# One layer of a retention and S5 decoder: projections' tail in the two-bank layout, the last pair without GpSimd additions, retention's first loads on ACT's queue

## The chip, the cores and the metric

The kernel runs on one core of one Trainium2 chip. The metric is the device time of one execution in microseconds (us), as the median of several runs. The engines are TensorE (PE in the profile, with its weight loads as PEld), VectorE (DVE), ScalarE (ACT), GpSimd (POOL) and SyncE (SP). SP, ACT and POOL each have a queue of their own for issuing transfers (DMAs).

## What is computed

One layer over 1032 tokens (1024 of a prompt, 8 single-token samples), in float32, width 2048:

```python
h = rmsnorm(x, g_pre)
q, k, v, za, ub, zb, ga, gb = split(h @ w_in)             # 2048 -> 6 x 1024 and 2 x 2048 columns
ya, s_ret_new = retention(q, k, v, pos, s_ret)            # 8 heads, chunks of 128
ya = (ya * silu(za)) @ w_pa
yb, s_re, s_im = s5(ub, ...)                              # diagonal SSM, gelu, GLU
yb = (yb * silu(zb)) @ w_pb
merged = sigmoid(ga) * ya + sigmoid(gb) * yb
out = merged @ w_out
y = x + rmsnorm(out, g_post)
```

## The kernel before

Everything on TensorE is float32-accurate: an operand is split into a high part (`whi`, the rounded copy, cast by ACT) and a low part (`wlo`, the difference, on DVE), and each product is the three matmuls high x high, high x low, low x high. Weights come in 256 KB quarters (128 x 512) on SP's queue.

**Block products (line 892).** The larger projections go by pairs of 128-row blocks, each pair by seven products (n = 0 to 6) of 24 matmuls with 258 columns. A product accumulates in an `acc` tile, which is two PSUM banks wide; there are three of them (pool `pst`, six banks) and two `misc` banks (pool `pms`). Of a step's seven products n=0 and n=2 share one tile, n=1, 3 and 5 another, n=4 and 6 the third. `evac_st` and `evac_p` empty them by ACT copies and DVE additions; results are called "11", "22", "21", "12". In the last stage, `w_pb` (kind "pb", p = 0 to 7), `gated` multiplies a result by its gate (`zz`), adds the part of `w_pa` (`pap_d`, in DRAM), and writes to `mg_d`. The addition has two forms: an ACT load of the part (`pp`) in `load_z` and an addition by an engine, or an accumulating DMA from `pap_d` onto the tile on POOL's queue and, LAG = 4 products later, the write to `mg_d`. For p > 1 it is the first form, on DVE, except p = 7, where "11", "22" and "21" are added by POOL.

**Retention (lines 1011 to 1100).** Its heads are worked off in slots between the block products of `w_in`'s last pairs. `ret_const` loads constants by POOL's queue (`col`, `mask`, `selr`), sets `mhalf` on DVE and casts `selr` to `sel` on DVE. Head 0's first transfers (`load_vk`: `vT`, 516 KB, and `kT`, two of 258 KB) are issued by POOL's queue when `head(0)` starts. PE transposes `vT` through `misc` banks (lines 1046 and 1049), and ACT copies them out (line 1047) and so frees the banks.

**Output projection (line 1620 on).** `psum_layout(("pmm", 5), ("pms", 3))` closes the PSUM pools of the block products and opens one of five single banks (`mm`) and one of three (`misc`). `out_rows` computes 16 row blocks of the last 392 tokens (the 48 matmuls of a block have 392 columns, lines 209 to 211). `out_tokens` computes five column blocks of 128 tokens (`c`), three in a first call and two in a second (`last`), in four groups (`g`) of 512 output columns: per group 16 steps k, in each of which every column does its three matmuls (line 1782); then `evac` takes each column: a Square with a sum on ACT (line 1725), and a product with the gain on DVE (`z<-mm`). An `out_rows` load of the merged rows (`z<-mg_d`, line 1651) is issued by ACT's queue.

The order on each engine is set by a scheduler that goes through the program with estimated times, so an edit can move neighbours on the same engine. Tiles are released as a whole: who writes a tile anew waits for every reader of its last use, and closing a pool waits for all of its tiles.

Of the kernel before, what the change touches and what calls it, by code (L numbers as in the profile page):

```python
# [10 lines left out]
F32 = mybir.dt.float32  # L11
# [10 lines left out]
TOK = SEQ + NB  # L22
# [56 lines left out]
def emit(ctx, tc, I, O):  # L79
    nc = tc.nc  # L80
    V, A, P, T = nc.vector, nc.scalar, nc.gpsimd, nc.tensor
# [7 lines left out]
    def add(out, a, b, eng=None):  # L89
        return tt(out, a, b, ALU.add, eng)  # L90
# [22 lines left out]
    def psum_layout(*pools):  # L113
        if "stack" in banks_of:
            banks_of.pop("stack").close()
            banks_of.clear()
        st = banks_of["stack"] = ExitStack()
        for name, bufs in pools:
            banks_of[name] = st.enter_context(tc.tile_pool(name=name, bufs=bufs, space=PSUM))
# [93 lines left out]
    def mmbank(name="mm"):  # L213
        if "pst" in banks_of:
            return banks_of["pst"].tile([128, 2, 512], F32, name="acc")[:, 0, :]
        return banks_of["pmm"].tile([128, 512], F32, name="mm")

    def misc():
        return banks_of["pms"].tile([128, 512], F32, name="misc")
# [657 lines left out]
    acc = {}  # L877
# [130 lines left out]
    K = {}  # L1008

    def ret_const():  # L1010
        for n, shape in (("col", [128, 4, H]), ("mask", [128, 128])):
            K[n] = rp.tile(shape, F32, name=n)
            P.dma_start(K[n], I[n])
        K["mhalf"] = rp.tile([128, 8], F32, name="mhalf")
        V.memset(K["mhalf"], -0.5)
        selr = rp.tile([128, 64], F32, name="selr")
        P.dma_start(selr, I["sel"])
        K["sel"] = rp.tile([128, 8, 8], F32R, name="sel")
        V.tensor_copy(K["sel"], selr.rearrange("p (b c) -> p b c", b=8))
        K["a"] = act.tile([128, 2, TOK], F32, name="a12")  # L1020
        K["b"] = act.tile([128, 2, TOK], F32, name="a13")

    R = lambda name, shape, bufs=1, dt=F32: rp.tile(shape, dt, name=name, bufs=bufs)

    def load_vk(h):
        vT, kT = R("vT", [128, TOK]), R("kT", [128, TOK], 2)
        P.dma_start(vT, v_d[h])
        for a in range(2):
            P.dma_start(kT[64 * a:64 * a + 64], kq_d[0, h // 2, a, 64 * (h % 2):64 * (h % 2) + 64])
        return vT, kT  # L1030

    def head(h):
# [1 line left out]
        sq = lambda t: t[:, 0:1024].rearrange("p (a b) -> p a b", a=8)  # L1034
        qT, st = K["a"][:, 0], sq(K["a"][:, 1])
        vt, s0 = sq(K["b"][:, 0]), sq(K["b"][:, 1])
        vT, kT = K.pop("next") if h else load_vk(h)
        for a in range(2):
            P.dma_start(qT[64 * a:64 * a + 64], kq_d[1, h // 2, a, 64 * (h % 2):64 * (h % 2) + 64])
        if not h:  # L1040
# [445 lines left out]
    def load_z(s, name):  # L1486
        kind, p = steps[s]
        r, c = AT[name]
        zq[name] = zz_tile()
        A.dma_start(zq[name], (sga_d if kind == "pa" else sgb_d)[2 * p + r, :, HT * c:HT * c + HT])  # L1490
        if kind == "pb" and p > 1:
            zq[name, "p"] = ppp.tile([128, HT], F32, name="pp")
            A.dma_start(zq[name, "p"], pap_d[2 * p + r, :, HT * c:HT * c + HT])

    def gated(g, name, t, ps=None):
        s = g // 7
        kind, p = steps[s]
        r, c = AT[name]
        m, cols = 2 * p + r, slice(HT * c, HT * c + HT)
        z = zq.pop(name)  # L1500
        if ps is None:
            mul(t, t, z)
        else:
            mul(two(t), ps, two(z))
        if kind == "pa":
            P.dma_start(pap_d[m, :, cols], t)
        elif (name, "p") in zq:
            add(t, t, zq.pop((name, "p")), P if p == 7 and name != "12" else V)
            if c and p > 5:
                last_t[m] = t  # L1510
            P.dma_start(mg_d[m, :, cols], t)
        else:
            P.dma_start(t, pap_d[m, :, cols], accum_op=ALU.add)
            at(g + LAG, lambda: P.dma_start(mg_d[m, :, cols], t))
# [104 lines left out]
    estack.close()  # L1619
    wstack.close()  # L1620
    stage_pool(SW, 3)
    psum_layout(("pmm", 5), ("pms", 3))
    zp = ctx.enter_context(tc.tile_pool(name="zp", bufs=1))
    stl = ctx.enter_context(tc.tile_pool(name="stl", bufs=2))
    wxp = ctx.enter_context(tc.tile_pool(name="wxp", bufs=1))
# [79 lines left out]
    def out_tokens(c0, nch, last):  # L1705
        if last:
            view = lambda t: t.rearrange("p (k c) -> p k c", k=4)
            more.extend(view(st_tile()) for _ in range(2))
        zt, slots, sm = {}, {}, {}
        zts[last] = zt  # L1710
        S = 512
        for c in range(nch):
            o = 8 * (c0 + c)
            sm[c] = small[:, o:o + 4], small[:, o + 4:o + 5], small[:, o + 5:o + 6], small[:, o + 6:o + 7]

        def x_of(g, c):
            o = (nch + (c if last else 0)) * S
            return zt[g][:, o:o + S]

        def load_x(g, c):  # L1720
            P.dma_start(x_of(g, c), I["xB"][c0 + c, :, S * g:S * g + S])

        def evac(g, c, ps):
            s4, r1, r2, r3 = sm[c]
            A.activation(misc(), ps, AF.Square, accum_out=s4[:, g:g + 1])
            mul(zt[g][:, c * S:c * S + S], ps, gb[:, S * g:S * g + S])
            if g == 2:
                add(r1, s4[:, 0:1], s4[:, 1:2])
                add(r1, r1, s4[:, 2:3])
                V.tensor_scalar(r1, r1, 1.0 / D, EPS, ALU.mult, ALU.add)  # L1730
                V.memset(r2, -0.5)
            if g == 3:
                V.scalar_tensor_tensor(r1, s4[:, 3:4], 1.0 / D, r1, ALU.mult, ALU.add)
                P.tensor_tensor(r3, r1, r2, ALU.pow)

        def finish(g, c, eng, x=None):
            z = zt[g][:, c * S:c * S + S]
            V.scalar_tensor_tensor(z, z, sm[c][3], x_of(g, c) if x is None else x, ALU.mult, ALU.add)
            eng.dma_start(O["yB"][c0 + c, :, S * g:S * g + S], z)

        RING = [0, 1, 2, 3, 1, 2, 3, 2, 3, (0,), (1,), 3]

        def place(i):
            p = RING[i]
            return zts[True][0][:, (2 + p[0]) * S:(3 + p[0]) * S] if isinstance(p, tuple) else zt[p][:, 3 * S:4 * S]

        def load_step(i):
            P.dma_start(place(i), I["xB"][c0 + i % 3, :, S * (i // 3):S * (i // 3) + S])  # L1750

        def finish_all():
            then = {1: (4,), 2: (5,), 3: (6,), 4: (9,), 5: (7, 10), 6: (8,), 8: (11,)}
            for i in range(12):
                g, c = divmod(i, 3)
                for _ in range(4):
                    yield
                finish(g, c, P, place(i))
                for n in then.get(i, ()):
                    load_step(n)  # L1760
                if i in (9, 10):
                    P.dma_start(place(i), I["xB"][c0 + 3 + i - 9, :, 0:S])
                if c == 2:
                    free.append(slots[g])

        order_w = deque((g, k) for g in range(4) for k in range(KD))
        w = {}
        for g in range(4):
            ps = [mmbank() if c < 2 else misc() for c in range(nch)]
            steps = [[(k, c) for c in range(nch)] for k in range(KD)]  # L1770
            if last and g == 3:
                steps[13:] = [[(k, c) for k in (13, 14, 15)] for c in range(nch)]
            for st in steps:
                for k, c in st:
                    while order_w and order_w[0] <= (g, k + 1):
                        gk = order_w.popleft()
                        w[gk] = wtile(I["w_outB"][gk])
                    wh, wl = (t.rearrange("p a b -> p (a b)") for t in w[g, k])
                    t = (c0 + c) * 128
                    xh, xl = (a[:, t:t + 128] for a in mg[k])  # L1780
                    for a, b in ((xh, wh), (xh, wl), (xl, wh)):
                        anchor["p"] = T.matmul(ps[c], a, b, start=k == 0 and a is xh and b is wh, stop=k == KD - 1 and a is xl).ins  # L1782
                    if k == KD - 1:
                        if c == 0:
                            slots[g] = free.popleft()
                            zt[g] = flat(slots[g])
                            if not last:
                                load_step(g)
                            elif g:
                                for cc in range(nch):  # L1790
                                    load_x(g, cc)
                        evac(g, c, ps[c])
                        if last and g == 3:
                            for gg in range(4):
                                finish(gg, c, A if gg % 2 else nc.sync)
                slot()
        if not last:
            bg.append(finish_all())
# [85 lines left out]
```

## Time and profile before

| what | us |
|---|---|
| median of 3 runs | 2610.0 (2609.98 to 2617.08) |
| profiled execution | 2613.67 |
| its span on the core | 2611.9 |
| PE busy | 2588.0 (99%) |
| DVE busy | 1856.4 (71%) |
| ACT busy | 956.0 (37%) |
| POOL busy | 688.8 (26%) |

The span is the time from the core's first to its last instruction in the profiled execution; 1.8 us of that execution lie outside it. The profile's page lists busy time by engine, the chain that ended last, and the costliest groups of instructions; the trace answers for any stretch what each engine ran, what it waited for (in square brackets behind an instruction: idle time before it and who released it), and the clock that TensorE was granted (1.00 is full speed).

### The profile page before, as it was taken

What the parts mean: (1) busy time and instruction counts of PE and PEld (TensorE: products, weight loads), DVE (VectorE), ACT (ScalarE), POOL (GpSimd) and SP (SyncE); (2) the same over time, 40 slices, a digit from 0 to 9 for tenths busy, and PEclk for the clock granted to TensorE, in tenths of its full rate; (3) what the DMA queues carried; (4) which work ended last, traced back from release to release, by engine and by line L of the source; (5) the groups of instructions that cost most, each with busy time, mean ns of one, the idle gap of its engine ahead of it and who ended that gap; (6) DMA issues with size and microseconds to landing.
All of it is one profiled execution on the core that took longest, in us unless ns stands there. A gap on an engine that the chain in (4) does not pass through costs nothing.

```text
span 2611.9 us, 51326 instructions
## 1 busy us (share of the span) xinstructions
PE 2588.0 (99%) x19652; PEld 2531.1 (97%) x19652; DVE 1856.4 (71%) x3872; ACT 956.0 (37%) x1679; POOL 688.8 (26%) x1137
## 2 busy tenths in 40 slices
PE   9999999999999999999999999999999999999998
PEld 8999999999999999999999999999999999998886
DVE  7655988898898877558877666666577878544555
ACT  6113232333323324443234444445332422443344
POOL 0103322222222222332234434333422221111011
PEclk9999999999999999999999999999999999999999
DMA  6896534444444447886778878778867786655666
GB/s 192 257 265 217 154 111 125 138 120 124 129 122 131 131 127 245 207 206 168 164 192 241 231 197 209 206 196 250 273 226 255 232 230 212 215 166 182 187 200 227
DMA packets 229909, 500.25 MB, mean 192 GB/s; under 512 B 32432, under 2 KB 54912, under 8 KB 229536
## 3 DMA queue, kind: packets, MB, share of 16 engines
q0 software_dynamic: 90352, 263.82, 36.2%
q1 hardware_dynamic: 103072, 179.57, 22.5%
q10 hardware_dynamic: 36240, 53.60, 7.0%
q8 instruction: 154, 2.52, 0.4%
q14 instruction: 91, 0.75, 0.1%
HBM read 340.57 MB, written 156.30 MB: 190 GB/s over the span
## 4 chain that ended last, share of the span: by engine, by line
PE 97%; DVE 1%; issue 1%; DMA 1%; ACT 0%; DVEq 0%; SPq 0%; POOLq 0%; POOL 0%; ACTq 0%
PE acc L892 65%; PE mm L1782 7%; PE mm L209 5%; PE mm L210 5%; PE mm L211 5%; PE misc L1782 2%; PE acc L209 1%; PE acc L210 1%; PE acc L211 1%; PE misc L634 1%; PE misc L712 1%; PE misc L711 1%; PE misc L1099 1%; PE misc L1089 1%; PE misc L1068 1%
## 5 line engine op out<-in xcount | busy, mean ns | idle before, releaser
L892 PE MATMUL acc<-a,whi 128*128 128x258 f32 x9632 | 1561.4, 284 | 1.0 <-ACT whi L873 0.6
L892 PEld LDWEIGHTS acc<-a,whi 128*128 128x128 f32 x9632 | 1325.8, 190 | 5.2 <-issue 2.6
L892 PE MATMUL acc<-a,wlo 128*128 128x258 f32 x4816 | 969.1, 282 | 0.0
L892 PEld LDWEIGHTS acc<-a,wlo 128*128 128x128 f32 x4816 | 744.7, 189 | 0.0
L84 DVE TENSOR_TENSOR wlo<-wraw,whi 128x512 fp32r<-128x512 f32 x482 | 332.0, 689 | 237.9 <-ACT whi L202 138.1
L873 ACT CAST whi<-wraw 128x512 fp32r<-128x512 f32 x344 | 213.5, 621 | 619.6 <-PE acc L892 481.1
L873 ACT CAST whi<-wr 128x512 fp32r<-128x512 f32 x258 | 160.0, 620 | 507.4 <-PE acc L892 445.3
L209 PE MATMUL mm<-a,whi 128*128 128x384 f32 (+2 forms) x704 | 234.2, 334 | 8.6 <-ACT whi L202 5.2
L210 PE MATMUL mm<-a,whi 128*128 128x384 f32 (+2 forms) x704 | 233.7, 332 | 0.0
L211 PE MATMUL mm<-a,wlo 128*128 128x384 f32 (+2 forms) x704 | 232.2, 330 | 0.0
L84 DVE TENSOR_TENSOR wlo<-wr,whi 128x512 fp32r<-128x512 f32 x273 | 187.2, 686 | 51.6 <-ACT whi L873 30.0
L1782 PE MATMUL mm<-whi,a 128*128 128x512 f32 x512 | 171.1, 395 | 0.0
L202 ACT CAST whi<-wraw 128x512 fp32r<-128x512 f32 x138 | 85.5, 620 | 208.2 <-PE mm L210 104.1
L209 PEld LDWEIGHTS mm<-a,whi 128*128 128x128 f32 x704 | 133.6, 190 | 9.2 <-ACT whi L202 5.2
L211 PEld LDWEIGHTS mm<-a,wlo 128*128 128x128 f32 x704 | 133.9, 190 | 0.4 <-DVE wlo L84 0.2
L210 PEld LDWEIGHTS mm<-a,whi 128*128 128x128 f32 x704 | 133.3, 189 | 0.4 <-DVE a L363 0.4
L84 DVE TENSOR_TENSOR wraw<-wr 128x512 f32<-128x512 f32 x172 | 118.1, 686 | 2.9 <-DMA wr<-in_w_pa 0.6
L1782 PEld LDWEIGHTS mm<-whi,a 128*128 128x128 f32 x512 | 96.1, 188 | 22.8
L84 DVE TENSOR_TENSOR p<-acc,p 128x516 f32<-128x516 f32 x86 | 59.6, 692 | 70.9 <-PE acc L892 70.7
L84 DVE TENSOR_TENSOR wlo<-wx,whi 128x512 fp32r<-128x512 f32 x76 | 52.5, 692 | 71.4 <-ACT whi L202 71.1
L84 DVE TENSOR_TENSOR u<-acc,u 128x516 f32<-128x516 f32 x86 | 59.7, 694 | 60.0 <-PE acc L892 58.7
L84 DVE TENSOR_TENSOR u<-acc,p 128x516 f32<-128x516 f32 x86 | 59.5, 692 | 59.0 <-PE acc L892 58.7
(374 smaller groups left out, 3449.3 us busy)
## 6 DMA issues: line engine op xcount, KB each, us to landing
wr<-in_w_in SPq DMA_DIRECT2D x280, 256.0 KB
pt_d<-u POOLq DMA_DIRECT2D x70, 258.0 KB, 3.2
u<-pt_d POOLq DMA_DIRECT2D x70, 258.0 KB, 5.3
wraw<-in_w_outB SPq DMA_DIRECT2D x66, 256.0 KB
stg<-fm_d POOLq DMA_DIRECT2D x44, 258.0 KB, 4.5
wx<-in_w_outB SPq DMA_DIRECT2D x43, 256.0 KB
wraw<-in_w_out SPq DMA_DIRECT2D x39, 256.0 KB
pt_d<-st POOLq DMA_DIRECT2D x35, 258.0 KB, 3.3
```

The source lines that it names most:

```text
L84: return (eng or V).tensor_tensor(out, a, b, op)
L202: anchor["a"] = A.copy(hi, raw).ins
L209: T.matmul(ps, wh[:, i, :], xh[:, t0:t1], start=first, stop=False)
L210: T.matmul(ps, wh[:, i, :], xl[:, t0:t1], start=False, stop=False)
L211: anchor["p"] = T.matmul(ps, wl[:, i, :], xh[:, t0:t1], start=False, stop=last).ins
L634: T.matmul(ps[0:16, g * 128:(g + 1) * 128], B1[:, g, :], W3[:, g, 0:8, :], start=True, stop=True)
L711: T.matmul(o, Tm[:, g, :], U[:, g, 0:136], start=True, stop=False)
L712: T.matmul(o, W3[:, g, 1:9, :], X[:, g, 0:136], start=False, stop=True)
L873: anchor["a"] = A.copy(hi, f).ins
L892: anchor["p"] = T.matmul(ps[:, j, 0:258], a[:, i, :], b[:, 258 * j:258 * j + 258], start=first and i == 0 and a is wh and b is xh, stop=n ...
L1068: T.matmul(ps[:, c * 128:(c + 1) * 128], kt[:, 4 * i + c, :], vt[:, 4 * i + c, :], start=True, stop=True)
L1782: anchor["p"] = T.matmul(ps[c], a, b, start=k == 0 and a is xh and b is wh, stop=k == KD - 1 and a is xl).ins
```

## The change

Three edits.

1. Retention: `ret_const` allocates `a12` and `a13` first and issues head 0's `vT` and `kT` loads, by ACT's queue; `head(0)` takes them from there. On POOL's queue the three transfers are gone from behind `selr`.
2. Last pair (p = 7) of the "pb" products: "11" and "21" have no `pp` load any more and take the accumulating DMA on POOL's queue, with the write to `mg_d` four products later; "22" is added on DVE, as "12" was.
3. Output projection: the PSUM pools stay as they were (three `acc` tiles of two banks, two `misc` banks). In `out_rows` a block uses one bank of an `acc` tile. In `out_tokens` columns 0 and 1 share an `acc` tile, and column 2 has one of its own; in the first call the last two steps (k = 14, 15) go column by column; in the last group of the second call column 1 has its own tile.

```diff
     def ret_const():
+        K["a"] = act.tile([128, 2, TOK], F32, name="a12")
+        K["b"] = act.tile([128, 2, TOK], F32, name="a13")
+        K["next"] = load_vk(0, A)
         for n, shape in (("col", [128, 4, H]), ("mask", [128, 128])):
...
         V.tensor_copy(K["sel"], selr.rearrange("p (b c) -> p b c", b=8))
-        K["a"] = act.tile([128, 2, TOK], F32, name="a12")
-        K["b"] = act.tile([128, 2, TOK], F32, name="a13")
...
-    def load_vk(h):
+    def load_vk(h, eng=P):
         vT, kT = R("vT", [128, TOK]), R("kT", [128, TOK], 2)
-        P.dma_start(vT, v_d[h])
+        eng.dma_start(vT, v_d[h])
         for a in range(2):
-            P.dma_start(kT[64 * a:64 * a + 64], kq_d[0, h // 2, a, 64 * (h % 2):64 * (h % 2) + 64])
+            eng.dma_start(kT[64 * a:64 * a + 64], kq_d[0, h // 2, a, 64 * (h % 2):64 * (h % 2) + 64])
...
-        vT, kT = K.pop("next") if h else load_vk(h)
+        vT, kT = K.pop("next")
...
-        if kind == "pb" and p > 1:
+        if kind == "pb" and p > 1 and (p < 7 or c):
             zq[name, "p"] = ppp.tile([128, HT], F32, name="pp")
...
-            add(t, t, zq.pop((name, "p")), P if p == 7 and name != "12" else V)
+            add(t, t, zq.pop((name, "p")), V)
...
-    psum_layout(("pmm", 5), ("pms", 3))
...
-            ps = [mmbank() if c < 2 else misc() for c in range(nch)]
+            both_ = banks_of["pst"].tile([128, 2, 512], F32, name="acc")
+            ps = [both_[:, 0, :], both_[:, 1, :]]
+            if nch == 3:
+                ps.append(mmbank())
             steps = [[(k, c) for c in range(nch)] for k in range(KD)]
             if last and g == 3:
+                ps[1] = mmbank()
                 steps[13:] = [[(k, c) for k in (13, 14, 15)] for c in range(nch)]
+            elif not last:
+                steps[14:] = [[(k, c) for k in (14, 15)] for c in range(nch)]
```

How this moves instructions, at three places. On DVE where retention starts, before (`u_16992` is product n=1's result, `u_17059` that of n=3; the `wlo` behind `mhalf` is the low half of n=3's weights):

```order
L84 TENSOR_TENSOR wlo<-wr,whi 128x512
L1015 MEMSET mhalf 128x8
L84 TENSOR_TENSOR wlo<-wraw,whi 128x512
L84 TENSOR_TENSOR wraw<-wr,wraw 128x512
L84 TENSOR_TENSOR wraw<-wr 128x512
L84 TENSOR_TENSOR u_16992<-p_16932,acc 128x516
L84 TENSOR_TENSOR wlo<-wraw,whi 128x512
L84 TENSOR_TENSOR wraw<-wraw,wr 128x512
L1019 CAST sel<-selr 128x64
L84 TENSOR_TENSOR wlo<-wr,whi 128x512
```

The same place after:

```order
L84 TENSOR_TENSOR wlo<-wr,whi 128x512
L1018 MEMSET mhalf 128x8
L84 TENSOR_TENSOR u_16992<-p_16932,acc 128x516
L1022 CAST sel<-selr 128x64
L84 TENSOR_TENSOR wlo<-wraw,whi 128x512
L84 TENSOR_TENSOR wraw<-wr,wraw 128x512
L84 TENSOR_TENSOR wlo<-wraw,whi 128x512
L84 TENSOR_TENSOR wraw<-wr 128x512
L84 TENSOR_TENSOR wlo<-wr,whi 128x512
```

The low half of n=3's weights stood ahead of the cast of `selr` and now stands behind it.

On PE where the output projection starts, with the semaphores that an instruction waits for, before:

```order
L892 MATMUL acc<-a_26229,whi 128x258 x4
L892 MATMUL acc<-a_26229,wlo 128x258 x2
L209 MATMUL mm<-a_27795,whi 128x392 [waits DVE_49,Activation_49]
L210 MATMUL mm<-a_27795,whi 128x392
L211 MATMUL mm<-a_27795,wlo 128x392
L209 MATMUL mm<-a_27836,whi 128x392
```

The same place after:

```order
L892 MATMUL acc<-a_26229,whi 128x258 x4
L892 MATMUL acc<-a_26229,wlo 128x258 x2
L209 MATMUL acc<-a_27795,whi 128x392 [waits PE_49,Activation_49]
L210 MATMUL acc<-a_27795,whi 128x392
L211 MATMUL acc<-a_27795,wlo 128x392 [waits DVE_49]
L209 MATMUL acc<-a_27836,whi 128x392
```

The order is the same; the first matmul's wait for DVE is gone, and the third has one, for its own `wlo`.

On PE at the end of the first `out_tokens` group, before (`mm_29419`, `mm_29420` and `misc_29421` are columns 0, 1 and 2; a14 and a15 are the steps k = 14 and 15):

```order
L1782 MATMUL misc_29421<-whi_29671,a14_28123 128x512
L1782 MATMUL mm_29419<-whi_29687,a15_28120 128x512
L1782 MATMUL mm_29419<-wlo_29688,a15_28120 128x512
L1782 MATMUL mm_29419<-whi_29687,a15_28120 128x512
L1782 MATMUL mm_29420<-whi_29687,a15_28120 128x512
L1782 MATMUL mm_29420<-wlo_29688,a15_28120 128x512
L1782 MATMUL mm_29420<-whi_29687,a15_28120 128x512
```

After (`acc_29407` holds columns 0 and 1, `acc_29408` column 2, `acc_29715` the next group's columns 0 and 1):

```order
L1788 MATMUL acc_29407<-whi_29674,a15_28115 128x512
L1788 MATMUL acc_29408<-whi_29658,a14_28118 128x512
L1788 MATMUL acc_29408<-wlo_29659,a14_28118 128x512
L1788 MATMUL acc_29408<-whi_29658,a14_28118 128x512
L1788 MATMUL acc_29408<-whi_29674,a15_28115 128x512
L1788 MATMUL acc_29408<-wlo_29675,a15_28115 128x512
L1788 MATMUL acc_29408<-whi_29674,a15_28115 128x512
L1788 MATMUL acc_29715<-whi_29719,a0_27795 128x512
L1788 MATMUL acc_29407<-whi_29658,a14_28118 128x512
L1788 MATMUL acc_29407<-wlo_29659,a14_28118 128x512
L1788 MATMUL acc_29407<-whi_29658,a14_28118 128x512
```

Between column 0's last matmul (the first row) and column 1's steps k = 14 and 15, which write the tile that column 0's evacuation reads, there are now six matmuls of column 2 and one of the next group.

## Rows read from the trace of the kernel before

**Rows 1.** The page: PE's busy time, and the chain that ended last by engine.

```profile
PE 2588.0 (99%) x19652; PEld 2531.1 (97%) x19652; DVE 1856.4 (71%) x3872; ACT 956.0 (37%) x1679; POOL 688.8 (26%) x1137
PE 97%; DVE 1%; issue 1%; DMA 1%; ACT 0%; DVEq 0%; SPq 0%; POOLq 0%; POOL 0%; ACTq 0%
```

**Rows 2.** What PE waited for, by line of the waiting instruction: us in total, times, longest. The other entries are of 0.6 us and less.

```profile
PE mm L209 <- ACT whi L202: 5.2, 1, 5.2
PE mm L209 <- DVE u L84: 2.8, 1, 2.8
PE misc L1049 <- ACT a L1047: 2.2, 1, 2.2
```

**Rows 3.** PE where retention starts: start us, duration us, instruction, and in brackets the idle time before it and its releaser.

```profile
1361.51 0.65 PE L892 MATMUL acc<-a,whi 128*128 128x258 f32 x4
1362.00 0.40 PE L892 MATMUL acc<-a,wlo 128*128 128x258 f32 x2
1362.23 0.64 PE L892 MATMUL acc<-a,whi 128*128 128x258 f32 x4
1365.11 0.27 PE L1049 MATMUL misc<-ident,vT 128*8 128x128 f32 x1 [2.23 <-ACT a L1047]
```

**Rows 4.** ACT in the same stretch.

```profile
1346.04 0.58 ACT L982 COPY p<-acc 128x516 f32<-128x516 f32 x1
...
1362.65 1.28 ACT L966 ACT_TABLE_LOAD   x1 [2.16 <-DMA st<-pt_d]
...
1364.49 1.06 ACT L1047 COPY a<-misc 128x512 f32<-128x512 f32 x2
```

**Rows 5.** DVE in the same stretch.

```profile
1347.47 0.07 DVE L1015 MEMSET mhalf<- 128x8 f32 x1 [3.35 <-DMA kq_d<-pl]
1347.54 0.69 DVE L84 TENSOR_TENSOR wlo<-wraw,whi 128x512 fp32r<-128x512 f32 x1
...
1352.67 0.20 DVE L1019 CAST sel<-selr 128x64 fp32r<-128x64 f32 x1 [1.06 <-DMA selr<-in_sel]
1352.78 0.68 DVE L84 TENSOR_TENSOR wlo<-wr,whi 128x512 fp32r<-128x512 f32 x1
1354.36 0.70 DVE L84 TENSOR_TENSOR u<-acc,p 128x516 f32<-128x516 f32 x1 [0.89 <-PE acc L892]
```

**Rows 6.** DMA issues of 1336 to 1366 us: tiles, queue, count, KB each, median us from issue to landing.

```profile
kq_d<-pl POOLq DMA_DIRECT2D x3, 258.0 KB, 4.7
...
vT<-v_d POOLq DMA_DIRECT2D x1, 516.0 KB, 6.9
...
st<-pt_d POOLq DMA_DIRECT2D x1, 258.0 KB, 9.9
...
selr<-in_sel POOLq DMA_DIRECT2D x1, 32.0 KB, 3.7
```

**Rows 7.** Four stretches by window: from and to, length, busy us (instructions) of PE, PEld, DVE, ACT and POOL, granted clock, DMA share, GB/s. They are the stretch of rows 3, the idle time ahead of the output projection, its first matmuls, and one in the middle of `out_tokens`.

```profile
1360.00:1366.00 6.00, 3.77 (x33) 3.56 (x32) 1.57 (x3) 3.37 (x5) 1.39 (x3) 1.00 1.01 294
2231.80:2234.80 3.00, 0.24 (x2) 0.03 (x1) 3.00 (x5) 1.04 (x2) 2.08 (x2) 1.00 0.07 26
2234.80:2238.60 3.80, 3.73 (x12) 3.76 (x13) 2.81 (x5) 0.00 (x0) 0.54 (x1) 0.55 0.65 215
2450.00:2500.00 50.00, 50.00 (x218) 40.52 (x217) 18.85 (x33) 16.75 (x31) 0.54 (x1) 1.00 0.48 137
```

**Rows 8.** PE where the output projection starts, columns as in rows 3.

```profile
2231.64 0.40 PE L892 MATMUL acc<-a,wlo 128*128 128x258 f32 x2
2234.87 0.48 PE L209 MATMUL mm<-a,whi 128*128 128x392 f32 x1 [2.83 <-DVE u L84]
...
2238.64 0.34 PE L209 MATMUL mm<-a,whi 128*128 128x392 f32 x1
2238.81 0.34 PE L210 MATMUL mm<-a,whi 128*128 128x392 f32 x1
```

**Rows 9.** DVE ahead of that place and at it.

```profile
2224.65 1.04 DVE L84 TENSOR_TENSOR a<-mga,a 128x392 fp32r<-128x392 f32 x2
...
2228.13 2.14 DVE L84 TENSOR_TENSOR a<-mga,a 128x392 fp32r<-128x392 f32 x2
...
2232.36 1.76 DVE L84 TENSOR_TENSOR wlo<-wraw,whi 128x512 fp32r<-128x512 f32 x1
2234.04 0.68 DVE L84 TENSOR_TENSOR u<-acc,u 128x516 f32<-128x516 f32 x1
```

**Rows 10.** POOL and ACT there: the last addition on POOL, ACT's issue of the loads of merged rows, and ACT's first evacuation of `out_rows`.

```profile
2232.05 1.52 POOL L84 TENSOR_TENSOR p<-p,pp 128x516 f32<-128x516 f32 x1 [1.35 <-DVE p L84]
...
2241.31 0.85 ACTq L1651 DMA_DIRECT2D z<-mg_d  x2
...
2245.63 0.49 ACT L1675 ACTIVATE sp<-mm 128x392 f32<-128x392 f32 x1
```

**Rows 11.** The page's DMA issues, columns as in rows 6: the accumulating transfers of the block products (onto `u`, from `pt_d`).

```profile
u<-pt_d POOLq DMA_DIRECT2D x70, 258.0 KB, 5.3
```

**Rows 12.** The end of an `out_tokens` group: column 0's Square and the reading of its sum on ACT, and its product on DVE.

```profile
2475.57 0.58 ACT L1725 ACTIVATE misc<-mm 128x512 f32<-128x512 f32 x1
2476.06 0.19 ACT L1725 ACTIVATION_READ_ACCUMULATOR misc<-mm 128x1 f32 x1
...
2476.29 0.69 DVE L84 TENSOR_TENSOR z<-mm,z 128x512 f32<-128x512 f32 x1
```

## The prediction

> **What bounds the kernel now.** I read the page first: TensorE is busy for 2588.0 of 2611.9 us and the chain that ended last runs over it for 97% [rows 1]. So an edit pays only what it takes from PE's idle time, or from time at a lower clock. The waits of PE come next, since they name the few places where it stood still [rows 2]. The longest, 5.2 us, belongs to the first weights of the program, which no edit touches. The other two, 2.8 and 2.2 us, are the ones at which the change is aimed: closing the PSUM pools ahead of the output projection, and retention's first transposes. Then the stretches around both places, engine by engine [rows 3 to 11], and the end of a group of `out_tokens`, where PE has no idle time at all now and the change brings a new dependence [rows 7, 12].
>
> **Start of the output projection: a gain.** The last block product's final pair of matmuls starts at 2231.64 and the first matmul of `out_rows` at 2234.87, behind 2.83 us of idle time, released by DVE's `u<-acc,u` [rows 8]. That instruction is the last reader of the old pool; it came at 2234.04 because a `wlo` of 1.76 us stood ahead of it [rows 9]. After the gap the granted clock of the window is 0.55, that is, most of it at the lower level of 1.2 GHz: the 12 matmuls from 2234.87 to 2238.64 took 3.77 us [rows 7, 8]; at the pitch after them, 2238.64 to 2238.81, 12 would take 12 x 0.17 = 2.04. So this place costs 2.83 + (3.77 - 2.04) = 4.56 us.
>
> Without the closing, the first matmul waits only for its bank, long empty, and ACT's cast, which is done. What comes next is the third matmul, which needs `wlo`. In the trace that `wlo` ends at 2232.36 + 1.76 = 2234.12 [rows 9]. While POOL adds, from 2232.05 for 1.52 us [rows 10], it takes 1.76 instead of the usual 0.68 [rows 5, 9]; two `a<-mga` of 2228.13 take 2.14 where the same pair took 1.04 at 2224.65 [rows 9]. The change takes both POOL additions away (1.08 + 1.10 us of DVE's time) and puts one addition of about 0.6 on DVE. So `wlo` can end at about 2234.12 - 2.18 + 0.6 = 2232.5, against a need at 2231.9 + 2 x 0.17 = 2232.2. That leaves a wait of 0 to 0.5 us, too short next to 2.83 to expect a clock loss. I take -4.4 us; the bounds are -4.6 (no wait) and -3.0 (a wait of 0.5, and 1 us later for weights that arrive as late as now while PE is 4.6 us earlier).
>
> What is queued behind new waits there: ACT's issue of `z<-mg_d` waits for the last writes to `mg_d`, and two of these now come after an accumulating DMA. Behind it on ACT stand the first block's two evacuations and the cast of the second block's third quarter. `p` is ready at 2232.05 at the latest [rows 10]; an accumulating DMA took 5.3 [rows 11] and the write that follows has the size of a `kq_d<-pl`, 4.7 [rows 6]: 2242.0. PE wants that quarter at 2231.9 + 72 x 0.17 = 2244.1, and three ACT instructions of some 0.5 to 0.6 us [rows 10] are needed ahead, so 2242.4 is the deadline. It holds, barely; the price if it doesn't stands with the rivals. The two `pp` loads that go were on ACT's queue, where nothing waited for them: zero.
>
> **Start of retention: one wait exchanged for another.** PE now loses 2.23 us at line 1049 [rows 3], because ACT's copies out of `misc` stand behind a table load and an ACTIVATE that wait for `st<-pt_d` [rows 4], an accumulating DMA that took 9.9 us, behind `vT` and `kT` on POOL's queue [rows 6]. The clock in that stretch stayed at 1.00 [rows 7], so the loss is the wait. In the new order the table load (1.28 us) does not wait any more, and `vT` and `kT` are not ahead of `st`. Three `pl` loads are, directly behind `selr`, though. If `st` landed no earlier at all, 2.23 - 1.28 = 0.95 us would be left.
>
> But the DVE order brings a new wait. The low half of n=3's weights, done at 1347.54 + 0.69 now, stands behind the cast of `selr`, which started at 1352.67 when `selr` had landed [rows 5]. Product n=3 ends just ahead of 1354.36, when DVE takes it [rows 5], so with 24 matmuls at 0.12 us (six from 1361.51 to 1362.23 [rows 3]) it begins at about 1351.4 and needs `wlo` after four of them, at 1351.9. The cast (0.11 from its start to the next) and `wlo` (0.68) put it at 1353.5 at the earliest: a wait of 1.6 us. That holds if `selr` lands in 3.7 us as now. On ACT's queue `vT` and `kT`, 1 MB, now start before it. The nearest rows are `kq_d<-pl` with 4.7 and, as the upper bound, `vT` itself with 6.9 [rows 6], which would make the wait 2.6 or 4.8. I take 2.6, since 32 KB should not take longer than 258 KB do. Behind the cast DVE holds the weights of n=4 and 5 as well, but these have a product's time each. The wait at line 1049 and this one don't add: PE comes 2.6 us later to the transposes, and the 0.95 has gone into that. So the loss is 2.6 instead of 2.23 to 2.4 (start to start): +0.2 us. Bounds: 1.6 - 2.4 = -0.8, and 4.8 - 2.4 = +2.4, with 1.7 more if a wait that long brings the lower clock, as the 2.83 us one did and the 2.23 us one didn't [rows 7]: +4.1.
>
> The Trainium skill, page "DMA: Bandwidth & Descriptors", section "Queues, rings and completion order", says that each DMA engine goes round-robin between the queues, packet by packet. By that rule `selr` alternates with the other queue and would not be held for its whole megabyte; the wait would be near 1.6 and the sum near -4.8, and no row here shows which of the two holds, since both loads now share one queue.
>
> ACT's issue of `vT` waits for the last `kq_d<-pl`, landed at 1347.4 (DVE's MEMSET waits for it too [rows 5]). Behind it on ACT is `COPY p<-acc`, 0.58 us, which ran at 1346.04 [rows 4] and must end before n=2 writes that tile at 1351.4 - 2.9 = 1348.5. With some 0.3 for the issue it ends at 1348.3 or 1348.4: covered by 0.1 to 0.2 us, and a miss would only shift n=3 towards the same `selr`.
>
> **Groups of out_tokens: a small cost.** Columns 0 and 1 share a tile, so column 1's last matmuls wait until column 0 has been emptied. That takes, from the end of column 0's last matmul, some 0.1 to the Square, 0.68 for Square and read, and 0.69 for DVE's product [rows 12]: 1.5 to 1.6 us. In the first call six matmuls of column 2 and one of the next group cover it: 7 x 50/218 = 1.6 us [rows 7]. There are four such places, and three in the second call with a cover of ten matmuls, 2.3 us. At the margin, then: 0 to 0.2 at each of the seven; 0.4 together, between 0 and 1.5. Below zero is excluded: PE is gapless there now.
>
> **Sum.** -4.4 + 0.2 + 0.4 = -3.8 us. From 2613.7 of the profiled execution, 2609.9; from the median of 2610.0, **2606.2 us**. All that PE loses at both places is 4.56 + 2.4 = 7.0 us, which is 0.27%, below the 0.3% (7.8 us) that a measurement of this kernel can tell from no change.
>
> **Rivals.**
> (a) Both losses vanish and nothing replaces them, if `selr` lands in time after all: 2610.0 - 7.0 = 2603.0. For it: small transfer, engines with room. Against: DVE had to wait for `selr` until 1352.67 as it is. Chance 0.13.
> (b) `selr` is held by the megabyte ahead of it and the clock falls: +2.4 to +4.1 - 4.4 + 0.4, so 2608.4 to 2610. Chance 0.2.
> (c) Slower: the evacuations of `out_tokens` come late. DVE and ACT also split the weights, and each such instruction ahead of an evacuation (0.68 on DVE, 0.6 on ACT) takes the whole margin, which is 0.1 us. Both ahead at all seven places: 7 x 1.2 = 8.4 us, -4.4 + 0.2 + 8.4 = +4.2, so 2614. It decides from (4.4 - 0.2)/7 = 0.6 us per place. Against: at the place shown the evacuation started at once [rows 12]. Chance 0.12.
> (d) The output projection starts early but ACT stands in `z<-mg_d`: with an accumulating DMA of 9.9 us [rows 6] instead of 5.3 the issue is 4.6 later, PE waits 4 us, and the gain there is gone: 2610. Chance 0.08.
> (e) Each of the seven waits, however short, brings the lower clock, at the 1.7 us of the 2.83 us wait: 7 x 1.7 = 12 more, -3.8 + 12 = +8, so 2618. Against: a wait of 2.23 us left the clock at 1.00 [rows 7]. Chance 0.02. The Trainium skill, page "TensorE: Matmul & The Clock Gate", section "A second HAM failure mode: psum-queue depth-cycling", describes this: short idles between groups of matmuls at the turn of PSUM banks let the clock swing between its levels. The row of the 2.23 us wait doesn't bear it out here.
>
> **Chances.** The forecast, 2604.5 to 2607.5, has 0.45; the rivals as given. Faster by over 0.3% (under 2602.2) needs more than both waits, from a place that these rows don't show: 0.08. Slower by over 0.3% (over 2617.8) needs (e) or several of (b) to (d): 0.04. Within: 0.88. The range, 2602 to 2613, takes in (a), (b), (d) and part of (c).
>
> **What would show it.** In the profile after: no wait at line 209 for DVE `u`, and a granted clock of 1.00 right after it; a wait of 1.6 to 4.8 us of a line 892 matmul for DVE `wlo` at about 1352, which ends behind the cast of `selr`; none or a short one at line 1049; waits of the `out_tokens` matmuls for DVE `z` at the ends of groups, 0.2 us each at most. The forecast is wrong if `wlo` is in time at 1352, if the group ends show 0.6 us or more each, or if a new wait for ACT's casts stands near 2242.

## The result and the profile after

The changed kernel takes 2617.25 us in the median (2615.79 to 2618.57), the kernel before 2611.3 (12 runs of each). The ratio is 1.002 with a 95% interval of 1.0012 to 1.0029: some 5 us slower, where 3.8 us faster was forecast. The profiled execution took 2617.61, with a span of 2615.8 against 2611.9.

The first view is again what PE waited for, by line: us in total, times, longest.

```profile
PE mm L209 <- ACT whi L202: 6.0, 1, 6.0
PE acc L892 <- DVE wlo L84: 5.0, 1, 5.0
PE acc L892 <- ACT p L982: 0.8, 1, 0.8
PE acc L892 <- ACT whi L873: 0.6, 1, 0.6
PE acc L892 <- DVE u L84: 0.4, 2, 0.2
```

Both waits of [rows 2] at which the change aimed are gone. Two others have come, both at the start of retention: 5.0 us for a `wlo` and 0.8 us for ACT's copy of `p`. In the timeline of PE there (columns as in rows 3):

```profile
1349.37 0.75 PE L892 MATMUL acc<-a,whi 128*128 128x258 f32 x4 [0.83 <-ACT p L982]
...
1357.97 0.80 PE L892 MATMUL acc<-a,wlo 128*128 128x258 f32 x2 [4.97 <-DVE wlo L84]
1358.56 1.06 PE L892 MATMUL acc<-a,whi 128*128 128x258 f32 x4
1359.42 0.63 PE L892 MATMUL acc<-a,wlo 128*128 128x258 f32 x2
...
1362.43 0.97 PE L892 MATMUL acc<-a,whi 128*128 128x258 f32 x4
1363.24 0.41 PE L892 MATMUL acc<-a,wlo 128*128 128x258 f32 x2
...
1371.62 0.27 PE L1050 MATMUL misc<-ident,vT 128*8 128x128 f32 x1
```

Four matmuls took 0.64 us in [rows 3] and take 1.06 at 1358.56. The windows (columns as in rows 7) show the granted clock: it fell to 0.50 while PE still stood idle, and the matmuls after it ran at the lower level of 1.2 GHz until about 1363: the four at 1362.43 took 0.81 us to the next start, those at 1358.56 took 0.86, and four take 0.48 at full speed.

```profile
1354.00:1356.40 2.40, 0.00 (x0) 0.00 (x0) 0.00 (x0) 0.72 (x2) 0.90 (x2) 0.98 1.01 236
1356.40:1362.40 6.00, 4.43 (x20) 4.43 (x21) 3.90 (x7) 0.11 (x1) 0.55 (x1) 0.50 1.03 328
```

What DVE did meanwhile, beside [rows 5]:

```profile
1348.21 0.07 DVE L1018 MEMSET mhalf<- 128x8 f32 x1 [4.11 <-DMA kq_d<-pl]
1349.35 0.69 DVE L84 TENSOR_TENSOR u<-p,acc 128x516 f32<-128x516 f32 x1 [1.07 <-ACT p L982]
1357.12 0.20 DVE L1022 CAST sel<-selr 128x64 fp32r<-128x64 f32 x1 [7.08 <-DMA selr<-in_sel]
1357.23 0.68 DVE L84 TENSOR_TENSOR wlo<-wraw,whi 128x512 fp32r<-128x512 f32 x1
```

For 7.08 us DVE waited at the cast, and `wlo` behind it, though its inputs were there: PE had begun with the high half of the same weights at 1352.36. The DMA issues of the same 30 us (columns as in rows 6) give the landings:

```profile
kq_d<-pl POOLq DMA_DIRECT2D x3, 258.0 KB, 5.9
...
mask<-in_mask POOLq DMA_DIRECT2D x1, 64.0 KB, 6.7
selr<-in_sel POOLq DMA_DIRECT2D x1, 32.0 KB, 7.4
col<-in_col POOLq DMA_DIRECT2D x1, 16.0 KB, 6.6
```

`selr` took 7.4 us, twice the 3.7 of [rows 6]; 16 KB took 6.6. What the queues moved from 1350.5 to 1355 us (packets, MB, share of the 16 DMA engines' time) suggests why; experiments 4 and 10 test it:

```profile
q10 hardware_dynamic: 270, 0.97, 88.2%
q0 software_dynamic: 98, 0.15, 15.5%
```

q10 is ACT's queue, with `vT` and `kT`; q0 is POOL's, with the small loads. In these 4.5 us 0.97 MB went by the one and 0.15 MB by the other. And ACT, which issued them, came late to the copy of `p`, because the issue of `vT` waited for `kq_d<-pl`, whose landing released DVE's MEMSET at 1348.21 too:

```profile
1348.30 0.33 ACTq L1028 DMA_DIRECT2D vT<-v_d  x1
1348.73 0.59 ACT L982 COPY p<-acc 128x516 f32<-128x516 f32 x1 [5.54 <-PE acc L892]
```

It ran at 1346.04 before [rows 4]. The bracket of COPY names PE, which had been done since 1345.5; the issue above it was what held ACT.

At the start of the output projection the forecast came true. PE's timeline, beside [rows 8]:

```profile
2238.34 0.40 PE L892 MATMUL acc<-a,wlo 128*128 128x258 f32 x2
2238.58 0.34 PE L209 MATMUL acc<-a,whi 128*128 128x392 f32 x1
...
2240.74 0.34 PE L209 MATMUL acc<-a,whi 128*128 128x392 f32 x1
```

No idle time and full speed: the 13th matmul starts 2.16 us after the first, where it took 3.77 in [rows 8]. From the last product's row (2238.34 now, 2231.64 before) to that 13th matmul it is 2.40 us now, 7.00 before: 4.6 us gained.

Behind it something was lost, though, and no wait shows it. From the 13th matmul to the Square of the last group (the first row is of before, the second of after) it is 2597.79 - 2238.64 = 359.15 us before and 2601.72 - 2240.74 = 360.98 after:

```profile
2597.79 0.58 ACT L1725 ACTIVATE misc<-mm 128x512 f32<-128x512 f32 x1 [1.55 <-PE mm L1782]
```

```profile
2601.72 0.58 ACT L1725 ACTIVATE misc<-acc 128x512 f32<-128x512 f32 x1 [1.54 <-PE acc L1788]
```

So this stretch costs 1.83 us more. Matched matmul by matmul, all of it lies in `out_tokens`, spread over the seven group ends. At the first of them, on PE:

```profile
2413.39 0.62 PE L1788 MATMUL acc<-whi,a 128*128 128x512 f32 x2
2413.84 0.40 PE L1788 MATMUL acc<-wlo,a 128*128 128x512 f32 x1
2414.12 0.50 PE L1788 MATMUL acc<-whi,a 128*128 128x512 f32 x1
2414.46 0.40 PE L1788 MATMUL acc<-wlo,a 128*128 128x512 f32 x1
2414.69 0.84 PE L1788 MATMUL acc<-whi,a 128*128 128x512 f32 x3
```

The starts lie 0.28 and 0.34 us apart, where they should be 0.23. A matmul's modelled duration is 0.40, so a delay of 0.05 to 0.11 us between two starts leaves PE "busy" and appears in no list of waits. Summed over the group ends such steps (a start later than the 0.23 allows) come to 1.85 us.

### The profile page after: what moved, and what is told of

It reads as the page before. It is cut to its first block, busy times and chain, and to the rows that moved or that the text cites. A ratio compares the mean times of both kernels' runs of the same rounds, so it can differ in the third digit from the quotient of the medians.

```text
span 2615.8 us, 51329 instructions
## 1 busy us (share of the span) xinstructions
PE 2590.5 (99%) x19652; PEld 2530.4 (97%) x19652; DVE 1852.1 (71%) x3873; ACT 954.9 (37%) x1679; POOL 686.2 (26%) x1133
## 4 chain that ended last, share of the span: by engine, by line
PE 95%; DVE 2%; issue 1%; DMA 1%; ACT 1%; POOL 0%; DVEq 0%; POOLq 0%; ACTq 0%; SPq 0%
PE acc L892 64%; PE acc L1788 8%; PE acc L209 3%; PE acc L210 3%; PE acc L211 3%; PE mm L211 2%; PE mm L209 2%; PE mm L210 2%; PE misc L634 1%; DMA xr<-in_xT 1%; PE misc L712 1%; PE misc L711 1%; PE misc L1090 1%; PE misc L1100 1%; PE misc L1069 1%
## 5 line engine op out<-in xcount | busy, mean ns | idle before, releaser
L1788 PE MATMUL acc<-whi,a 128*128 128x512 f32 x640 | 202.0, 396 | 0.0
L209 PE MATMUL mm<-a,whi 128*128 128x384 f32 (+1 forms) x448 | 145.1, 326 | 6.0 <-ACT whi L202 6.0
L1788 PEld LDWEIGHTS acc<-whi,a 128*128 128x128 f32 x640 | 120.2, 188 | 30.3 <-DVE z L84 2.1
L209 PE MATMUL acc<-a,whi 128*128 128x392 f32 (+2 forms) x448 | 149.3, 333 | 0.0
L210 PE MATMUL acc<-a,whi 128*128 128x392 f32 (+2 forms) x448 | 148.8, 332 | 0.0
L211 PE MATMUL acc<-a,wlo 128*128 128x392 f32 (+2 forms) x448 | 147.9, 330 | 0.0
L211 PE MATMUL mm<-a,wlo 128*128 128x384 f32 (+1 forms) x448 | 145.1, 324 | 0.2
L210 PE MATMUL mm<-a,whi 128*128 128x384 f32 (+1 forms) x448 | 145.2, 324 | 0.0
L1788 PE MATMUL acc<-wlo,a 128*128 128x512 f32 x320 | 126.9, 397 | 0.0
```

The source lines that it names most:

```text
L209: T.matmul(ps, wh[:, i, :], xh[:, t0:t1], start=first, stop=False)
L210: T.matmul(ps, wh[:, i, :], xl[:, t0:t1], start=False, stop=False)
L211: anchor["p"] = T.matmul(ps, wl[:, i, :], xh[:, t0:t1], start=False, stop=last).ins
```

## Experiments

Theory 1: the loss is in retention; DVE stands in the cast of `selr` ahead of n=3's `wlo`, and `selr` lands late since a megabyte was issued ahead of it; the gain at the output projection is real, and 1.85 us of it go again in `out_tokens`. The rivals are named in the expectations. Each result gives the median, the ratio to the kernel before with its 95% interval, and the difference of the medians. The medians of the kernel before beside the experiments were 2611.35 (first four), 2611.6 (the next four) and 2611.46 (the last two).

**1. The retention part alone** (edit 1 of the change, on the kernel before).

> The kernel before with the retention part of the change alone (head 0's first loads lead, by ACT's queue). Theory 1, by the trace of the changed kernel: the whole loss sits here. ACT's copy of p is 1.1 us late behind the load of vT, the cast of selr holds n=3's low half for 5.4 us, the lower clock after it costs 2.1, and the old stall of 2.1 at the transposes goes: +6.5 us against the kernel before, about 2617.8. Theory 2 (the parts hurt one another, by the loads of the last pair or the scheduler's order): under +4 us here.

2619.52 us, ratio 1.0029 [1.0018, 1.0041]: +8.2 us. The interval, 4.7 to 10.7 us, holds the 6.5 of theory 1 and excludes theory 2. PE waited 6.28 us for `wlo`, 0.2 for `p`; `selr` took 8.7 us to land:

```profile
1358.44 0.80 PE L892 MATMUL acc<-a,wlo 128*128 128x258 f32 x2 [6.28 <-DVE wlo L84]
```

```profile
selr<-in_sel POOLq DMA_DIRECT2D x1, 32.0 KB, 8.7
```

**2. The change without the retention part.**

```diff
-        K["next"] = load_vk(0, A)
...
-        vT, kT = K.pop("next")
+        vT, kT = K.pop("next") if h else load_vk(h)
```

> The changed kernel with the retention part undone. Theory 1: the early start of the output projection is worth -4.6 us and the waits for shared tiles at seven places in out_tokens cost +1.85, so -2.7 us against the kernel before, about 2608.6, with the old stall of 2.2 us at retention's transposes back. Theory 2: the output projection's gain is smaller in time than in the trace: within 1 us of the kernel before.

2608.94 us, ratio 0.999 [0.9982, 0.9999]: -2.4 us, near the -2.7 of theory 1. The interval, -4.7 to -0.3 us, doesn't quite exclude theory 2; the trace does: the start of the output projection is 4.6 us shorter than in the kernel before, and the steps in `out_tokens` sum to 1.85. But the old stall, which it had expected back, was not in the profile: no wait at line 1049 at all. That led to the eighth experiment.

**3. The cast of `selr` later.**

```diff
-        V.tensor_copy(K["sel"], selr.rearrange("p (b c) -> p b c", b=8))
+        K["cast"] = lambda: V.tensor_copy(K["sel"], selr.rearrange("p (b c) -> p b c", b=8))
...
+        if not h:
+            K["cast"]()
         ps = misc()
         T.transpose(ps[0:8, 0:128], vT[:, SEQ:TOK], ident)
```

> The changed kernel, but the cast of selr is written behind the first transposes of head 0, so that on DVE it stands some ten instructions later. The transfers stay as they are. Theory 1 (it is the place of the cast on DVE): no wait of PE for wlo at 1352, no lower clock, the copy of p still 1.1 us late, no stall at the transposes since PE is later there and st has landed: -1.0 in retention, -4.6 + 1.85 behind: -3.8 us against the kernel before, about 2607.5. Theory 3 (the loads on ACT's queue disturb the stretch whatever DVE's order, by other late landings): a wait of 2 us or more stays there, so 2610 or more; selr lands after 7 us in both.

2610.46 us, ratio 0.9997 [0.9988, 1.0006]: 6.8 below the changed kernel. `selr` still took 7.8 us, and PE did not wait for `wlo`, nor did the clock fall. So the place of the cast carries most of the loss, some four fifths of the 8.3 us between the changed kernel and experiment 2. What kept it from 2607.5 is a wait of the old kind, at the transposes, and 0.4 us for `p`:

```profile
1364.35 0.27 PE L1052 MATMUL misc<-ident,vT 128*8 128x128 f32 x1 [1.58 <-ACT a L1048]
```

The granted clock in the window around it was 1.00 (columns as in rows 7):

```profile
1362.00:1368.00 6.00, 4.42 (x39) 4.21 (x38) 2.18 (x4) 3.48 (x6) 1.42 (x2) 1.00 0.84 216
```

**4. `selr` ahead of `vT` and `kT`, on ACT's queue.**

```diff
+        selr = rp.tile([128, 64], F32, name="selr")
+        A.dma_start(selr, I["sel"])
         K["next"] = load_vk(0, A)
...
-        selr = rp.tile([128, 64], F32, name="selr")
-        P.dma_start(selr, I["sel"])
```

> The changed kernel, but selr is loaded by ACT's queue, ahead of vT and kT; the cast keeps its place on DVE. Theory 1a (selr was held by the megabyte on ACT's queue): it lands within 3 us, at about 1351, wlo is ready in time, and the time is that of the late cast, about 2607.5. Theory 1b (a small transfer simply takes 7 us in this crowded stretch, whatever stands ahead of it): it lands at about 1355, and a wait of 3 us with a lower clock stays: 2612 to 2614.

2611.77 us, ratio 1.0002 [0.9993, 1.0011]: 5.5 below the changed kernel. Issued at 1348.20, `selr` was there at 1352.34, after 4.1 us, which is nearer to 1a (the run changes the queue of `selr` as well as its turn; experiment 10 keeps the queue):

```profile
1352.34 0.20 DVE L1022 CAST sel<-selr 128x64 fp32r<-128x64 f32 x1 [4.15 <-DMA selr<-in_sel]
```

The wait for `wlo` is gone. The time is that of 1b all the same, for other reasons: the cast did not keep its place, it now stands ahead of `u<-p,acc` on DVE, so that PE waits for this; and ACT issues one load more ahead of the copy of `p`:

```profile
1349.28 0.75 PE L892 MATMUL acc<-a,whi 128*128 128x258 f32 x4 [1.31 <-ACT p L982]
...
1353.28 0.71 PE L892 MATMUL acc<-a,whi 128*128 128x258 f32 x4 [0.84 <-DVE u L84]
```

**5. The last pair alone, without POOL's additions** (edit 2 of the change).

> The kernel before with the last pair's part alone: no additions on POOL; PSUM pools are closed and opened as before. Theory 1: DVE reaches the release of the old pool earlier, since nothing stretches its wlo; by the changed kernel's trace u<-acc,u ends 1.4 us behind the last product, so PE waits 1.5 us instead of 2.83 and the clock stays up: -3.0 us, about 2608.3 where the kernel before has 2611.3. Theory 2: the closing of the pools is what costs, and the DVE order around it keeps the wait at 2.5 us or more: within 1 us of the kernel before.

2609.18 us, ratio 0.9989 [0.998, 0.9997]: -2.4 us. PE waits 1.4 us less for the release of the old pool, as theory 1 said, and the clock stays up: the first 12 matmuls take 2.23 us, from 2232.69 to 2234.92.

```profile
2232.69 0.42 PE L209 MATMUL mm<-a,whi 128*128 128x392 f32 x1 [1.38 <-DVE u L84]
```

**6. The layout alone, with POOL's additions** (edit 3).

> The kernel before with the output projection's part alone: pools stay, POOL still adds in the last pair. Theory 1: the first two matmuls start at once, the third waits 1.9 us for a wlo stretched by POOL's addition, the clock stays up: -2.7 us at the start, +1.85 in out_tokens, together -0.8 us. Theory 2 (the release alone decides): no wait for wlo, -4.6 + 1.85 = -2.7 us.

2612.38 us, ratio 1.0003 [0.9994, 1.0012]: +0.8 us where -0.8 was expected; the interval, -1.6 to +3.1 us, holds both and excludes the -2.7 of theory 2. The trace has what theory 1 says: a wait for `wlo` with the clock at 1.00, and at the group ends the same 1.85 us.

```profile
2229.47 0.34 PE L210 MATMUL acc<-a,whi 128*128 128x392 f32 x1
2231.59 0.44 PE L211 MATMUL acc<-a,wlo 128*128 128x392 f32 x1 [1.77 <-DVE wlo L84]
```

```profile
2231.00:2235.00 4.00, 3.42 (x18) 3.22 (x19) 4.00 (x8) 2.13 (x4) 0.83 (x2) 1.00 0.40 139
```

So each of the two parts leaves a wait that only the other removes, and the layout alone loses in `out_tokens` most of what it gains ahead of it: 1.85 of 2.4 us.

**7. A tile for each column** (without the retention part).

```diff
-            both_ = banks_of["pst"].tile([128, 2, 512], F32, name="acc")
-            ps = [both_[:, 0, :], both_[:, 1, :]]
-            if nch == 3:
-                ps.append(mmbank())
+            ps = [mmbank() for c in range(nch)]
             steps = [[(k, c) for c in range(nch)] for k in range(KD)]
-            if last and g == 3:
-                ps[1] = mmbank()
+            if last and g == 3 or not last:
                 steps[13:] = [[(k, c) for k in (13, 14, 15)] for c in range(nch)]
-            elif not last:
-                steps[14:] = [[(k, c) for k in (14, 15)] for c in range(nch)]
```

> The changed kernel with the retention part undone, and in out_tokens every column has an acc tile of its own, with the last three steps column by column in the first call. Theory 1 (the 1.85 us in out_tokens come from column 1 sharing column 0's tile, and column 2 waiting for it): no step at the group ends, -4.6 us against the kernel before, about 2606.8. Theory 2 (they come from evacuations of 1.7 us on ACT and DVE, whichever the tile): steps of 0.1 to 0.3 us stay, about 2608.6.

2608.91 us, ratio 0.9991 [0.9982, 1.0]: -2.7 us; the interval, -4.7 to 0, holds both forecasts. The trace lies between the two: the steps at the group ends sum to 1.2 us instead of 1.85, in other places. The run changes two things at once, the tiles and the number of steps that go column by column; experiment 9 takes the second back.

**8. The kernel before, once more.**

> The kernel before, unchanged, for another profile. Theory 4 (the stall of 2.2 us at retention's transposes in the first profile is not there in a usual execution: that execution took 2613.7, 2.3 above the median of 2611.35, and the undone retention of the second experiment shows no such wait): no wait or a short one at line 1049, span about 2609.6. Theory 5 (it is always there): a wait of 2 us and a span of about 2612.

2611.35 us, span 2609.5. There is no wait at line 1049; what PE waited for was:

```profile
PE mm L209 <- ACT whi L202: 6.0, 1, 6.0
PE mm L209 <- DVE u L84: 2.8, 1, 2.8
PE acc L892 <- ACT whi L873: 0.6, 1, 0.6
PE acc L892 <- DVE u L84: 0.4, 2, 0.2
```

`st<-pt_d` landed in 7.6 us instead of the 9.9 of [rows 6]. Theory 4 holds for this execution. Over the seven profiles with untouched retention (the first, experiments 2, 5, 6, 7, 8 and 9) PE waited there for 2.2 us once, with `st` at 9.9 us, 0.7 once, with `st` at 8.2 (experiment 6), and not at all five times, with `st` at 5.9 to 7.7:

```profile
st<-pt_d POOLq DMA_DIRECT2D x1, 258.0 KB, 7.6
```

```profile
PE misc L1049 <- ACT a L1047: 0.7, 1, 0.7
```

The first row is of experiment 8, the second of experiment 6.

**9. A tile for each column, the last two steps by column** (against the kernel of the seventh experiment).

```diff
-            if last and g == 3 or not last:
-                steps[13:] = [[(k, c) for k in (13, 14, 15)] for c in range(nch)]
+            n = 13 if last and g == 3 else 14
+            steps[n:] = [[(k, c) for k in range(n, KD)] for c in range(nch)]
```

> As the seventh experiment (no retention part, own acc tile for every column), but only the last two steps go column by column, in both calls. Theory 1 (what was left there, 1.2 us at the group ends, came from weights that the grouped steps want too early and from the second call's ungrouped ends): no step above 0.1 us at the group ends, span 1.0 us shorter than there, -4.4 us against the kernel before. Theory 2 (a tile is free only 1.7 us after its column ends, and three tiles don't cover that): steps of 0.1 us and more stay at every group, -3.4 us.

2607.72 us, ratio 0.9987 [0.9978, 0.9996]: -3.7 us, the lowest median of all, though 1.2 us from experiments 2 and 7 is within the noise. The interval, -5.7 to -1.0, holds both theories. The steps left sum to 0.5 us, at three places of 0.1 to 0.2 each, one of them in the second call. That is more than theory 1 allows and less than theory 2, which wanted steps at every group; the start of the output projection keeps its 4.6 us.

**10. `vT` and `kT` lead by POOL's queue** (the retention part alone, with `load_vk(0, P)`).

> The kernel before with head 0's vT and kT leading, as in the changed kernel, but by POOL's queue, so that selr stands behind the megabyte on its own queue; the scheduler puts the cast of selr behind n=3's result here, and ACT is not held. Theory 1 (what costs is the cast's place, not the late selr): selr lands after 6 us or more here too, and PE doesn't wait for wlo: within 1.5 us of the kernel before. Theory 3 (the lead itself disturbs the stretch): 3 us or more slower.

2612.08 us, ratio 1.0003 [0.9994, 1.0011]: +0.6 us. `selr` took 8.2 us, as long as behind the loads on ACT's queue, and DVE waited at the cast for 4.05 us, but at a place where PE had its weights:

```profile
selr<-in_sel POOLq DMA_DIRECT2D x1, 32.0 KB, 8.2
```

```profile
1353.31 0.70 DVE L84 TENSOR_TENSOR u<-acc,p 128x516 f32<-128x516 f32 x1 [1.78 <-PE acc L892]
1358.06 0.20 DVE L1022 CAST sel<-selr 128x64 fp32r<-128x64 f32 x1 [4.05 <-DMA selr<-in_sel]
1358.17 0.69 DVE L84 TENSOR_TENSOR wlo<-wraw,whi 128x512 fp32r<-128x512 f32 x1
```

Theory 1 again, and against theory 3: the interval ends at +2.9 us, and in the trace the lead and the late `selr` cost PE 0.4 us here, a wait for DVE's `u` behind the cast.

## Why the prediction was wrong

By its own steps:

- **Start of the output projection: right.** -4.4 was forecast, -4.6 came. The third matmul found its `wlo`, and ACT's issue of `z<-mg_d` held nobody up (no wait for ACT's casts stands there: rival d did not come). Experiments 5 and 6 show that both parts are needed: -3.0 and -2.4 us in the trace there, -4.6 together.
- **Start of retention: the failed step.** +0.2 was forecast with bounds of -0.8 and +4.1. The mechanism was the one described, the cast of `selr` ahead of n=3's weights, and the case was rival b. But the wait was 5.0 us in the changed kernel and 6.3 in experiment 1, not 2.6 nor at most 4.8, and the whole step cost 8.7 us (below). The sentence that failed is "32 KB should not take longer than 258 KB do": `selr` took 7.4 to 8.7 us wherever `vT` and `kT` went ahead, by ACT's queue or by its own, and 4.1 when it went first (experiments 1, 3, 4 and 10). In the changed kernel transfers of 16, 32 and 64 KB took 6.6 to 7.4 us and `kq_d<-pl` with 258 KB took 5.9: what was issued ahead mattered, not the size. POOL's queue, with the small loads, had 15.5% of the engines' time beside 88.2% for ACT's. The Trainium skill, page "DMA: Bandwidth & Descriptors", section "Queues, rings and completion order", has the engines take the queues in turn, packet by packet; the prediction read from it a wait near 1.6 us, and the trace, with its wait of 5.0, does not bear that reading out.
- **The clock** fell; the forecast had nothing for it, its upper bound 1.7 us. It cost 2.4: the 24 matmuls from 1357.97 to 1363.24 took 5.27 us and take 2.88 at 0.12.
- **ACT's copy of `p`** was called covered by 0.1 to 0.2 us. PE waited for it 0.2 to 1.3 us in four profiles (the changed kernel and experiments 1, 3 and 4), 0.8 in the changed kernel. That a miss "would only shift n=3 towards the same `selr`" was wrong as well: what holds ACT is the landing of `kq_d<-pl`, and POOL's loads of `selr` wait for the same landing, so both shift together.
- **The gain in retention was not there to be had.** The 2.23 us at line 1049 were subtracted, as 2.4, as a loss that every execution has. A usual execution does not have it: one profile of seven shows it (experiment 8), and that execution took 2613.67 beside a median of 2610.0. The prediction set both numbers side by side and went on from the difference as if it were spread over the whole run. How many of the unprofiled runs have the stall is not known.
- **Retention in sum.** Matched matmul by matmul with the profile of experiment 8, this stretch is 8.7 us longer in the changed kernel and 8.8 in experiment 1; it is 2.1 longer in experiment 3, 2.8 in experiment 4 and 0.5 in experiment 10. By terms the changed kernel has 0.8 + 5.0 for the waits, 2.4 for the clock and 0.4 where PE starts again after a wait: 8.6. The medians say 8.2 (experiment 1) and 8.3 (the change less experiment 2). From the forecast's +0.2 it is 2.4 more for the wait, 2.4 for the clock, 1.2 for `p` and the starts, and 2.4 for the gain that was not there. Rival b had the cause, and its highest price, +4.1, was less than half of it.
- **out_tokens: right in mechanism, mis-sized.** 0.4 was forecast, at most 1.5; 1.85 came. Of the first call's waits one kind was counted, column 1 for column 0's evacuation (0.15 at each of four places); column 2 of the next group, which waits for column 1's, adds 0.15 at two places; the change of calls costs 0.3, and the second call's ends, called covered, cost 0.27, 0.27 and 0.1. With a tile for each column and the last steps of both calls column by column, 0.5 of it is left (experiment 9); how the other 1.3 divides between the tiles and the order was not tested. Rival c named a price of 1.2 a place; it was 0.26 on average. The clock did not fall there (rival e): it was granted at 1.00 in every window of 50 us from 2250 to 2600.

The sum, against a usual execution: +8.7 - 4.6 + 1.8 = +5.9 us; the medians differ by 5.95, and the ratio of all runs gives 5.2 (3.1 to 7.6).

What stays open is why `st<-pt_d` lands after 5.9 us in one profile and 9.9 in another with the same retention code; and the steps of 0.5 us left in experiment 9 were not followed up.

## What to carry to other kernels

Before a stall is counted as a gain, take a second profile, above all when the profiled execution is slower than the median by about the stall's length. When an edit moves transfers, look for the instruction on a busy engine that waits for a small one behind them. Here 1 MB issued ahead, on the same queue or another, made 32 KB land some 4 to 5 us later, which is about what the 1 MB itself takes (an estimate: 4.8 us, at the 0.97 MB that ACT's queue moved in 4.5 us); and everything in order behind the waiting instruction is delayed too. Either the waiting instruction or the transfer can be moved: here the first gave back 6.8 us (experiment 3) and the second 5.5 (experiment 4).

## What the runs showed of the hardware

A 32 KB load took 3.3 to 4.3 us where no large transfer was issued just ahead of it (seven profiles, and experiment 4) and 7.4 to 8.7 us behind 1 MB (the changed kernel, experiments 1, 3 and 10). With 1 MB on ACT's queue, POOL's queue moved 0.15 MB in 4.5 us, with 15.5% of the engines' time. TensorE's granted clock fell to 0.50 inside the idle time of 4.97 us, and the matmuls behind it ran at that level, 1.2 GHz, from 1357.97 to about 1363. After 2.83 us of idle time it was down too [rows 7]; after 2.23 us [rows 7], 1.77 (experiment 6), 1.58 (experiment 3) and 1.38 us (experiment 5) TensorE ran on at 2.4 GHz.
